# Eight weight-transfer buffers beside the experts in place of six

## The chip, the cores and the metric

The kernel runs on one core of one Trainium2 chip. The time is device microseconds (us) for one execution. Engines are named as in the profile: PE (TensorE matmul), PEld (its weight loads), DVE (VectorE), ACT (ScalarE), POOL (GpSimd) and SP (SyncE, which here issues almost every transfer from device memory).

## What is computed

The reference runs two models one behind the other on a sequence of 256 tokens of width 1024, all in float32. The first block has two layers of attention and a mixture of experts with 32 experts, two of them per token:

```python
def step(acc, ew):
    w1e, w3e, w2e, ge = ew
    h = jax.nn.silu(xt @ w1e) * (xt @ w3e)
    return acc + ge[:, None] * (h @ w2e).astype(f32), None
y, _ = lax.scan(step, jnp.zeros((t, d), f32), (w1, w3, w2, gates.T))
```

Its result feeds the second block: two layers of a hybrid mixer (attention beside a state-space scan) and a gated feed-forward part, on the latent tokens and on 256 context tokens ("ctx"). The context part of layer 0, and the context states of layer 1, do not depend on the first block:

```python
out_l, out_c = hybrid_mixer(h_l, h_c, ..., update_ctx)   # mixer: projections, attention, two scans
x_ctx = x_ctx + g1_c * rmsnorm(m_c, norm_mix_post[l])    # only for l = 0
f_c = rmsnorm(x_ctx, norm_ffn_pre[l]) * (1.0 + sc2_c) + sh2_c
x_ctx = x_ctx + g2_c * rmsnorm(swiglu(f_c, w_gate[l], w_up[l], w_down[l]), norm_ffn_post[l])
```

## The kernel before

**Stages.** The program computes attention of the first block's layer 0 (to about 195 us of the profile), that layer's experts (about 205 to 795), attention of layer 1 (to about 985), its experts (about 990 to 1700), and then the second block on the latent tokens ("the tail", to 2475). A routing step ahead of each expert stage sorts the experts by their number of tokens. A flag chooses at run time between two versions of the stage. The profiled execution takes the one called with `fast` true; only that one is spoken of here.

**An expert stage.** It runs over ten units. A unit is a tile of 128 token slots with one to four experts. For each, `gather` builds a selection matrix `P` on DVE (out of `eq`) and multiplies the tokens `xh`, `xl` by it on PE in two halves of 16 products (`xgp`), each copied by ACT into one half of `xg`. Then `up` runs `h<-wch,xg` for `w1` and again for `w3`, `act` makes `g`, `down` turns `g` on PE (`gtp`), copies it on DVE to `gT`, runs `o<-wch,gT` with `w2`, and adds the result to the tokens by a matrix `St` (`yp`, then `y`). The tiles `gT` and `St` have two buffers each, `eq` has one of its own, and `tmp` (also `tj`) has one.

**Beside the experts.** The ctx pass of the second block runs in pieces between the expert products: `step` is called behind each group of expert products and advances the generator `ctx_pass`. In layer 0 that is the mixer of ctx, in layer 1 its feed-forward part and the states of the next mixer. Its weights (`w_in`, `w_out`, `w_gate`, `w_up`, `w_down`) come through the same buffers as the experts' weights; ACT and DVE split each into two parts (`whi`, `wlo`, lines 152 and 154), and then its buffer is free.

**Transfer buffers.** All large weights come through buffers of [128, 2048] float32, 8 KB in each of 128 partitions or 1.05 MB. `chunk()` hands them out in turn: four of pool `wch`, two of pool `wchm`, which exists up to the end of the second expert stage. A buffer of expert weights is filled by two transfers of 512 KB, a buffer of the ctx pass by one of 1024 KB. SP issues them in program order, and each waits there until the products that read the buffer's former contents are done. So does whatever stands behind it on SP. The built program also names eight completion semaphores (DMAHW0 to DMAHW7), which the transfers use in turn: a transfer waits until the former one on its semaphore has landed. Between the transfers SP also loads the experts' ranks into registers (`value_load`, `TENSOR_LOAD order` in the program), each once a layer.

**Order.** The source gives the order of work and the dependences; a scheduler then sets the order of instructions on each engine, so buffers that are handed out otherwise can change that order.

**Tiles around it.** `res` holds two tiles of 8 KB, `xa` and `xb`. `xb` first holds the ctx input, in attention the sum `pre` (line 299; `x1` in `build`), and beside the experts `m`, the ctx pass's results. `X[0]` is the latent residual of the second block, written first behind the last expert stage; the scan of ctx uses half of it for `y`. `kept[l]` holds the keys, values and two scan states of ctx in layer l, four tiles. `xs` and `Bt` are the scan's inputs.

Of the kernel before, what the change touches and what calls it, by code (L numbers as in the profile page):

```python
# [6 lines left out]
F32 = mybir.dt.float32  # L7
F32R = mybir.dt.float32r
# [55 lines left out]
class Net:  # L64
    def __init__(self, tc, ins, out):
        self.tc, self.nc, self.I, self.out = tc, tc.nc, ins, out
        self.stack = ExitStack()
        self.consts = self.pool("consts")
        self.wch = self.pool("wch", 4)
        self.more = None  # L70
        self.turn = 0
        self.behind = []

# [28 lines left out]


    def chunk(self):
        self.turn = (self.turn + 1) % 3
        p = self.more if self.more is not None and self.turn == 0 else self.wch
        return p.tile([128, 2048], F32, name="wch", tag="wch")

    def row(self, pool, src, name):
        n = src.shape[-1]  # L110
# [470 lines left out]
    def setup2(self):  # L581
        nc, cp, I = self.nc, self.consts, self.I
        V = nc.vector

        self.tri = cp.tile([128, 2, 128], F32, name="tri")
        V.tensor_scalar(self.tri[:, 0], self.iota_f, self.iota_p, None, op0=OP.is_ge)
        V.tensor_scalar(self.tri[:, 1], self.iota_f, self.iota_p, None, op0=OP.is_le)
        self.mask = cp.tile([128, 2, 128], BF, name="mask")
        V.tensor_scalar(self.mask, self.tri, 1.0, -NEG, op0=OP.subtract, op1=OP.mult)
        self.identb = cp.tile([128, 128], BF, name="identb")  # L590
        V.tensor_copy(self.identb, self.ident)
        self.bo = cp.tile([128, 2], F32, name="bo")
        V.tensor_scalar(self.bo[:, 1:2], self.iota_p, 63.5, None, op0=OP.is_gt)
        V.tensor_scalar(self.bo[:, 0:1], self.iota_p, 63.5, None, op0=OP.is_lt)
        self.cols = cp.tile([128, 2, 180], F32, name="cols2")
        nc.gpsimd.dma_start(self.cols, I["c_cols"].rearrange("l p c -> p l c"))
        self.rc = cp.tile([128, 2], F32, name="rcx")
        self.mods = [cp.tile([128, 48, 2], F32, name=f"mod{l}") for l in range(2)]
        self.X = [cp.tile([128, 8, 256], F32, name=f"X{s}") for s in range(2)]
        self.kept = [{"kn": cp.tile([128, 256], F32, name=f"kn{l}"), "v": cp.tile([128, 2, 128], F32, name=f"v{l}"),  # L600
                      "st": [cp.tile([128, 512], F32, name=f"st{l}{d}") for d in range(2)]} for l in range(2)]

    def transpose_in(self, ps, src, s):
        nc = self.nc
# [318 lines left out]
    def mixer(self, l, s, e, m, states_only=False):  # L923
# [24 lines left out]
        mp = self.pool(e.name + f"m{l}", stack=ms)  # L948
# [67 lines left out]
            exps.append(A.activation(dte, dte, AF.Exp).ins)  # L1016


        bc = mp.tile([128, 2, 2, 256], F32, name="bc", tag="bc")
        BT, CT = bc[:, 0], bc[:, 1]  # L1020
        Bt = mp.tile([128, 2, 2, 128], F32, name="Bt")
        xs = mp.tile([128, 2, 512], F32, name="xs")

        def conv(c0, p, out, dst):

# [60 lines left out]
        p = self.gemm2(e, w_in(1280 + 512), h, second=e.second, late=lag)  # L1086
# [3 lines left out]
        for c in range(2):  # L1090
            xc = e.tmp().rearrange("p (k t) -> p k t", k=2)
            p = self.gemm2(e, w_in(1280 + 256 * c), h, second=e.second)
# [3 lines left out]
        if not states_only:  # L1096
            p = self.gemm2(e, w_in(1280 + 768), h, second=e.second)
# [135 lines left out]
        if not states_only:  # L1233

            zs = self.X[0][:, 4:8].rearrange("p (t k) c -> p t (k c)", t=2) if s else mp.tile([128, 2, 512], F32, name="zs")
            for c in range(2):
                ws = self.block(e, w_in(768 + 256 * c))
                p = e.bank("acc", [128, 2, 256])
# [10 lines left out]
        if s:  # L1249
            kn, v = kept["kn"], kept["v"]  # L1250
        else:
            kn = mp.tile([128, 256], F32, name="kn")
            v = mp.tile([128, 2, 128], F32, name="v")
        kvw = self.block(e, w_in(512))
        p = e.bank("acc", [128, 512])
# [13 lines left out]
        if not states_only:  # L1269
# [4 lines left out]
            for c in range(2):  # L1274
                p = self.gemm2(e, w_in(c * 256), h)
# [91 lines left out]
        if m is None:  # L1367
            m = mp.tile([128, 8, 256], F32, name="m1")
        ss = None
        for c in range(4):  # L1370
            p = self.gemm2(e, ("w_out_2", l, 0, 8, c * 256), (ch, cl), order=(4, 5, 6, 7, 0, 1, 2, 3))
# [149 lines left out]
    def experts(self, l, r, xh, xl, y, norm, fast, bg):  # L1521
# [3 lines left out]
        nm = f"moe{l}{'f' if fast else 'g'}"  # L1525
        with ExitStack() as es:
            rp = self.pool(nm + "r", stack=es)
            wk = self.pool(nm + "w", 2, stack=es)
            ps = self.pool(nm + "p", 1, PSUM, stack=es)
            step = bg(es)  # L1530

            sc = r.sc if fast else self.slots(r, rp, False)
            cols = r.cols
# [58 lines left out]

            def gather(t):
                P = wk.tile([128, 2, 128], F32R, name="P", tag="P", bufs=1)
                eq = wk.tile([128, 2, 128], F32, name="eq", tag="eq", bufs=1)
                for tt in range(2):
                    V.tensor_scalar(eq[:, tt], self.iota_f, sc[:, 0, tt, t:t + 1], None, op0=OP.is_equal)
                    V.scalar_tensor_tensor(P[:, tt], self.iota_f, sc[:, 1, tt, t:t + 1], eq[:, tt], op0=OP.is_equal, op1=OP.add)
                xg = wk.tile([128, 8, 128], F32, name="xg", tag="xg", bufs=2 if fast else 3)
                for k0 in range(0, 8, 4):  # L1600
                    p = ps.tile([128, 512], F32, name="xgp", tag="o", bufs=no)
                    for k in range(4):
                        o = p[:, k * 128:(k + 1) * 128]
                        for i, (tt, part) in enumerate(((0, xh), (0, xl), (1, xh), (1, xl))):
                            PE.matmul(o, part[:, tt, k0 + k, :], P[:, tt], start=i == 0, stop=i == 3, skip_group_check=True)  # L1605
                    A.copy(xg[:, k0:k0 + 4, :], p.rearrange("p (k t) -> p k t", k=4))  # L1606
                return xg
# [31 lines left out]
            def down(u, gs_, final):  # L1639
                ts, parts = u  # L1640
                gTs, Ss, gates = [], [], []
                for t, g in zip(ts, gs_):
                    p = ps.tile([128, 512], F32, name="gtp", tag="t", bufs=1)
                    for j in range(4):
                        PE.transpose(p[:, j * 128:(j + 1) * 128], g.rearrange("s (p j) -> s j p", j=4)[:, j], self.ident)
                    gT = wk.tile([128, 4, 128], F32, name="gT", tag="gT")
                    V.tensor_copy(gT, p.rearrange("p (j s) -> p j s", j=4))
                    gTs.append(gT)
                    St = wk.tile([128, 256], F32R, name="St", tag="St")
                    tmp = wk.tile([128, 256], F32, name="tmp", tag="tmp", bufs=1)  # L1650
                    b = 128.0 * t
                    V.tensor_scalar(tmp, rows[:, 0], b, None, op0=OP.is_equal)
                    V.scalar_tensor_tensor(St, rows[:, 1], b, tmp, op0=OP.is_equal, op1=OP.add)
                    gc = wk.tile([128, 3], F32, name="gc", tag="gc")
                    for j in range(2):
                        tj = wk.tile([128, 256], F32, name="tj", tag="tmp", bufs=1)
                        V.scalar_tensor_tensor(tj, rows[:, j], b, rows[:, 2 + j], op0=OP.is_equal, op1=OP.mult,
                                               accum_out=gc[:, j:j + 1])
                    V.tensor_tensor(out=gc[:, 2:3], in0=gc[:, 0:1], in1=gc[:, 1:2], op=OP.add)
                    Ss.append(St)  # L1660
                    gates.append(gc[:, 2:3])
# [3 lines left out]
                for j0 in range(0, 4, nr):  # L1665
                    cs = load(w2v, ranks, slice(j0, j0 + nr), D)
                    first = together([lambda i=i, j=j, dh=dh, k=k, o=o, n=n: PE.matmul(  # L1667
                        os2[dh][i][o:o + n], gTs[i][:, j0 + j, o:o + n], cs[k][:, j, dh * 512:(dh + 1) * 512],
                        start=j0 + j == 0, stop=j0 + j == 3, skip_group_check=True)
                        for i in range(len(ts)) for j in range(nr) for dh in range(2) for k, o, n in reversed(parts)])  # L1670
# [18 lines left out]
            for i, u in enumerate(units):  # L1689
# [6 lines left out]
                    xgs = [gather(t) for t in units[i + 1][0]]  # L1696
                down(u, gs_, i == len(units) - 1)
            step(None)


M_BANKS = {"acc": ("acc", 2), "tr": ("acc", 2), "tp": ("acc", 2), "s": ("acc", 2), "ar": ("acc", 2), "y": ("acc", 2), "yi": ("acc", 2),
# [5 lines left out]
def build(tc, ins, out):  # L1707
    net = Net(tc, ins, out)
    nc = tc.nc
    V, A, PE = nc.vector, nc.scalar, nc.tensor  # L1710
    with net.stack:
        tail = ExitStack()
        with ExitStack() as first:
            res = net.pool("res", stack=first, side="right")
            x = res.tile([128, 2, 1024], F32, name="x", tag="xa")
            for tt in range(2):
                nc.sync.dma_start(x[:, tt], ins["x"][0, tt * 128:(tt + 1) * 128, :])
            cx = res.tile([128, 2, 1024], F32, name="cx", tag="xb")
            net.more = net.pool("wchm", 2, stack=first, side="right")
            net.setup()  # L1720
            net.setup2()
            fnorm = None
            for l in range(2):
                with ExitStack() as es:
                    with ExitStack() as right:
# [6 lines left out]
                        mp = net.pool(f"moe{l}", stack=es)  # L1732
# [23 lines left out]
                        (nc.gpsimd if tt else V).tensor_tensor(out=xl[:, tt], in0=src, in1=f(xh[:, tt]), op=OP.subtract)  # L1756
                    y = res.tile([128, 2, 1024], F32, name="y", tag="xa")
                    A.activation(y, x1, AF.Copy, scale=ALPHA)
                    m = res.tile([128, 8, 256], F32, name="m", tag="xb")

                    def ctx_pass(e):

# [36 lines left out]
                    with cmp.Else():  # L1799
                        net.experts(l, r, xh, xl, y, fnorm, False, lambda es: lambda first, n=0: None)  # L1800
                        with ExitStack() as es2:
                            e = net.env(f"d{l}", es2, T_BANKS, 6, 2)
# [2 lines left out]
                                pass  # L1805
                net.ln_finish(fnorm)
                x = y
            net.more = None

            e = net.env("t", tail, T_BANKS, 12, 4, {"raw": 3, "xdt": 2})  # L1810
            e.other = net.mod_units(1, 8, 24, e.tmp, lambda n: e.bank(n, [128, 512]), True)
            g, b = (net.cols[:, 1, 164 + 8 * i:172 + 8 * i] for i in range(2))
# [21 lines left out]
        with tc.tile_pool(name="ops", bufs=4, space=PSUM) as ps:  # L1834
            for tt in range(2):
                for k0 in range(0, 8, 4):
                    p = ps.tile([128, 512], F32, name="otp", tag="tp")
# [81 lines left out]
```

## Time and profile before

| | before |
|---|---|
| runs | 2459.08, 2465.37, 2470.23 us (median 2465.37) |
| profiled execution, its own time | 2476.79 us |
| its span | 2475.0 us |
| PE busy | 2167.9 us (88%) |
| PEld busy | 1633.0 us (66%) |
| DVE busy | 1097.7 us (44%) |
| ACT busy | 788.5 us (32%) |
| moved from and to device memory | 648.32 MB, mean 262 GB/s |

The span is the time from the first to the last record of the profiled execution; its own time is 1.8 us longer. Busy shares are means over stages that are unlike each other: attention and tail are mostly products, the expert stages are where most of the bytes come in. 744 transfers of 512 KB are expert weights.

### The profile page before, as it was taken

How to read it: one execution, taken by the hardware profiler on the slowest of the kernel's cores; microseconds unless marked ns; L12 is line 12 of the kernel's file. 1: busy time of each engine (PE TensorE's matmuls, PEld its weight loads, DVE VectorE, ACT ScalarE, POOL GpSimd, SP SyncE). 2: the span in 40 equal slices, each digit the busy share in tenths (PEclk: the TensorE clock that was granted, in tenths of full speed). 3: DMA queues.
4: the chain of work that ended last, by engine and by line, in shares of the span. 5: the costliest groups of instructions: out<-in, count | busy, mean ns of one | idle time of the engine just before them, and what ended most of it. 6: DMA issues, size and time to landing. Idle time of an engine off the chain costs nothing.

```text
span 2475.0 us, 40772 instructions
## 1 busy us (share of the span) xinstructions
PE 2167.9 (88%) x16468; PEld 1633.0 (66%) x16468; DVE 1097.7 (44%) x2031; ACT 788.5 (32%) x1309; POOL 143.8 (6%) x133
## 2 busy tenths in 40 slices
PE   7998888788875898798988878787999999999998
PEld 7885444334342887565554545456988998988998
DVE  4456332234322535432323223437755554765553
ACT  4344211122210454312221112214444443634442
POOL 2111000000001121000000000002000001100000
PEclk9998889999998899899999899998999998999999
DMA  9758999999999550999999989895326656405652
GB/s 296 241 170 275 396 345 353 397 409 385 366 356 352 165 170 23 328 365 337 383 377 383 360 320 372 320 361 180 109 68 188 188 175 194 150 5 170 188 179 77
DMA packets 353823, 648.32 MB, mean 262 GB/s; under 512 B 20637, under 2 KB 254181, under 8 KB 352080
## 3 DMA queue, kind: packets, MB, share of 16 engines
q1 hardware_dynamic: 347168, 638.65, 72.2%
q0 software_dynamic: 2288, 6.76, 1.0%
q8 instruction: 133, 2.18, 0.4%
q10 hardware_dynamic: 4160, 0.13, 0.1%
q14 instruction: 74, 0.61, 0.1%
HBM read 644.41 MB, written 1.06 MB: 261 GB/s over the span
## 4 chain that ended last, share of the span: by engine, by line
PE 60%; DMA 17%; issue 14%; DVE 5%; ACT 2%; SPq 1%; POOL 1%; ACTq 0%; DVEq 0%; POOLq 0%
DMA wch<-in_moe_w_dram 16%; PE acc_ps L166 9%; PE acc_ps L167 8%; PE acc_ps L168 8%; PE h L1627 6%; PE o L1667 3%; PE xgp L1605 3%; PE pj L166 3%; PE pj L168 3%; PE pj L167 3%; PE s_ps L1304 1%; PE o_ps L1332 1%; SPq L1565 1%; PE acc_ps L724 1%; PE modmo L643 1%
## 5 line engine op out<-in xcount | busy, mean ns | idle before, releaser
L154 DVE TENSOR_TENSOR wlo<-wch,whi 128x1024 fp32r<-128x1024 f32 (+1 forms) x333 | 403.3, 1213 | 602.1 <-ACT whi L152 579.4
L152 ACT CAST whi<-wch 128x1024 fp32r<-128x1024 f32 x342 | 351.8, 1033 | 720.5 <-PE acc_ps L167 497.2
L1627 PE MATMUL h<-wch,xg 128*32 128x512 f32 (+1 forms) x2368 | 347.6, 668 | 117.2 <-DMA wch<-in_moe_w_dram 117.0
L166 PE MATMUL acc_ps<-hh,whi 128*128 128x256 f32 x1360 | 391.0, 287 | 0.0
L167 PE MATMUL acc_ps<-hl,whi 128*128 128x256 f32 x1360 | 385.7, 284 | 0.0
L168 PE MATMUL acc_ps<-hh,wlo 128*128 128x256 f32 x1360 | 383.9, 282 | 0.0
L166 PEld LDWEIGHTS acc_ps<-hh,whi 128*128 128x128 f32 x1360 | 260.3, 191 | 29.1 <-issue 25.7
L1627 PEld LDWEIGHTS h<-wch,xg 128*32 128x32 f32 (+1 forms) x2368 | 78.7, 118 | 297.7 <-issue 146.0
L167 PEld LDWEIGHTS acc_ps<-hl,whi 128*128 128x128 f32 x1360 | 260.1, 191 | 4.5 <-issue 4.1
L168 PEld LDWEIGHTS acc_ps<-hh,wlo 128*128 128x128 f32 x1360 | 259.4, 191 | 0.8 <-issue 0.4
L1667 PE MATMUL o<-wch,gT 128*32 128x512 f32 (+1 forms) x1184 | 164.0, 635 | 40.7 <-DMA wch<-in_moe_w_dram 39.4
L166 PE MATMUL acc_ps<-ah,whi 128*128 128x256 f32 x528 | 150.7, 285 | 0.0
L167 PE MATMUL acc_ps<-al,whi 128*128 128x256 f32 x528 | 149.5, 283 | 0.0
L168 PE MATMUL acc_ps<-ah,wlo 128*128 128x256 f32 x528 | 148.5, 281 | 0.0
L1667 PEld LDWEIGHTS o<-wch,gT 128*32 128x32 f32 (+1 forms) x1184 | 38.7, 115 | 117.4 <-issue 66.2
L166 PEld LDWEIGHTS acc_ps<-ah,whi 128*128 128x128 f32 x528 | 101.1, 191 | 14.2 <-issue 14.1
L167 PEld LDWEIGHTS acc_ps<-al,whi 128*128 128x128 f32 x528 | 101.3, 192 | 0.0
L168 PEld LDWEIGHTS acc_ps<-ah,wlo 128*128 128x128 f32 x528 | 101.0, 191 | 0.1
L1684 DVE TENSOR_TENSOR y<-y,yp 128x512 f32<-128x512 f32 x80 | 54.6, 686 | 98.9 <-PE yp L1682 98.7
L1605 PE MATMUL xgp<-P,xh 128*128 128x128 f32 x320 | 81.8, 295 | 12.4 <-ACT xg L1606 9.1
L1605 PEld LDWEIGHTS xgp<-P,xh 128*128 128x128 f32 x320 | 65.6, 205 | 30.3 <-ACT xg L1606 23.1
L166 PE MATMUL pj<-xh,whi 128*128 128x256 f32 x256 | 75.6, 296 | 6.0 <-DVE xl L235 4.4
(728 smaller groups left out, 3801.2 us busy)
## 6 DMA issues: line engine op xcount, KB each, us to landing
wch<-in_moe_w_dram SPq DMA_DIRECT2D x744, 512.0 KB, 8.5
wch<-in_w_mod_dram SPq DMA_DIRECT2D x48, 1024.0 KB, 5.3
wch<-in_w_gate_dram SPq DMA_DIRECT2D x33, 1024.0 KB, 6.5
wch<-in_w_up_dram SPq DMA_DIRECT2D x33, 1024.0 KB, 5.6
wch<-in_w_in_dram SPq DMA_DIRECT2D x25, 1024.0 KB, 7.7
wch<-in_w_down_dram SPq DMA_DIRECT2D x24, 1024.0 KB, 5.2
wch<-in_moe_w_dram SPq DMA_DIRECT2D x12, 1024.0 KB, 10.0
wch<-in_w_out_dram SPq DMA_DIRECT2D x12, 1024.0 KB, 5.3
```

Source lines behind the costliest of these rows:

```text
L152: self.copied = nc.scalar.copy(hi, wk).ins
L154: self.halved = E.tensor_tensor(out=lo, in0=wk, in1=f(hi), op=OP.subtract).ins
L166: PE.matmul(out, ah, bh, start=first, stop=False, skip_group_check=True)
L167: PE.matmul(out, ah, bl, start=False, stop=False, skip_group_check=True)
L168: return PE.matmul(out, al, bh, start=False, stop=last, skip_group_check=True).ins
L643: PE.matmul(p[32 * g:32 * g + 32, (c % 2) * 256:(c % 2) * 256 + 256], self.sc[:, 4 * i + g, :], w[:, 4 * i + g, :], start=i == 0, stop=i = ...
L724: self.nc.tensor.matmul(p[:, j], ws[k][a][:, j * 128:(j + 1) * 128], act[b][:, k], start=n + k + j == 0, stop=n == 2 and k == 7, skip_grou ...
L1304: PE.matmul(ss_[c][:, i * 256:(i + 1) * 256], qn[r, j, qt * 128:(qt + 1) * 128], kk[r, :], start=True, stop=True, skip_group_check=True)
L1605: PE.matmul(o, part[:, tt, k0 + k, :], P[:, tt], start=i == 0, stop=i == 3, skip_group_check=True)
L1627: first = together([lambda i=i, q=q, k=k, o=o, n=n: PE.matmul(hs[i][o:o + n], xgs[i][:, k0 + q, o:o + n], cs[k][:, q, :], start=k0 + q == ...
L1667: first = together([lambda i=i, j=j, dh=dh, k=k, o=o, n=n: PE.matmul(os2[dh][i][o:o + n], gTs[i][:, j0 + j, o:o + n], cs[k][:, j, dh * 512 ...
L1684: V.tensor_tensor(out=ys, in0=ys, in1=yp, op=OP.add)
```

## The change

`chunk()` now goes through a list `ring` of places. Up to the end of the second expert stage it has six entries, as before: four times pool `wch`, and `m0` and `m1`. Within the fast version of an expert stage two more are appended, a tile of a new pool and the tile `xb` of `res`, and the turn starts over at the first entry; behind the stage the list has six entries again. In the tail it holds `wch` alone, as before.

To make room, `m` lies in `X[0]`; in layer 0 of the ctx pass `xs` and `Bt` lie in the tiles that will keep layer 1's scan states, keys and values, which become one tile each; in the fast version `gT` and `St` have one buffer each, and `eq` shares the buffer of `tmp`.

```diff
-        self.more = None
+        self.ring = [(self.wch, "wch")]
...
     def chunk(self):
-        self.turn = (self.turn + 1) % 3
-        p = self.more if self.more is not None and self.turn == 0 else self.wch
-        return p.tile([128, 2048], F32, name="wch", tag="wch")
+        self.turn += 1
+        pool, tag = self.ring[self.turn % len(self.ring)]
+        return pool.tile([128, 2048], F32, name="wch", tag=tag)
...
-        self.kept = [{"kn": cp.tile([128, 256], F32, name=f"kn{l}"), "v": cp.tile([128, 2, 128], F32, name=f"v{l}"),
-                      "st": [cp.tile([128, 512], F32, name=f"st{l}{d}") for d in range(2)]} for l in range(2)]
+        self.kept = []
+        for l in range(2):
+            kv = cp.tile([128, 2, 256], F32, name=f"kv{l}")
+            st = cp.tile([128, 2, 512], F32, name=f"states{l}")
+            self.kept.append({"kv": kv, "kn": kv[:, 0], "v": kv[:, 1].rearrange("p (t e) -> p t e", t=2), "both": st,
+                              "st": [st[:, d] for d in range(2)]})
...
+        xs = self.kept[1]["both"] if s and not states_only else mp.tile([128, 2, 512], F32, name="xs")
         BT, CT = bc[:, 0], bc[:, 1]
-        Bt = mp.tile([128, 2, 2, 128], F32, name="Bt")
-        xs = mp.tile([128, 2, 512], F32, name="xs")
+        if s and not states_only:
+            Bt = self.kept[1]["kv"].rearrange("p t (g n) -> p t g n", g=2)
+        else:
+            Bt = mp.tile([128, 2, 2, 128], F32, name="Bt")
...
             step = bg(es)
+            usual = self.ring
+            if fast:
+
+                deep = self.pool(nm + "d", 1, stack=es)
+                self.ring = usual + [(deep, "d"), (self.res, "xb")]
+                self.turn = -1
...
-                eq = wk.tile([128, 2, 128], F32, name="eq", tag="eq", bufs=1)
+                eq = wk.tile([128, 2, 128], F32, name="eq", tag="tmp", bufs=1)
...
-                    gT = wk.tile([128, 4, 128], F32, name="gT", tag="gT")
+                    gT = wk.tile([128, 4, 128], F32, name="gT", tag="gT", bufs=1 if fast else 2)
...
-                    St = wk.tile([128, 256], F32R, name="St", tag="St")
+                    St = wk.tile([128, 256], F32R, name="St", tag="St", bufs=1 if fast else 2)
...
             step(None)
+            self.ring = usual
...
-            net.more = net.pool("wchm", 2, stack=first, side="right")
+            more = net.pool("wchm", 1, stack=first, side="right")
+            net.ring = [(net.wch, "wch")] * 4 + [(more, "m0"), (more, "m1")]
...
-                    m = res.tile([128, 8, 256], F32, name="m", tag="xb")
+                    m = net.X[0]
...
-            net.more = None
+            net.ring = [(net.wch, "wch")]
```

What the change does to the order of instructions is seen at two places. The first is SP's queue at the start of layer 0's experts. Before, six buffers are asked for (two of the first experts, one of `w_in`, three more), and the rank loads follow:

```order
L1565 DMA wch_2505<-in_moe_w1_dram 128x1024
L1565 ISA
L1565 DMA wch_2516<-in_moe_w1_dram 128x1024
L1565 ISA
L1565 DMA wch_2516<-in_moe_w1_dram 128x1024
L1555 TENSOR_LOAD order_2013
L1555 ISA x2
L1555 TENSOR_LOAD order_2013
L1555 ISA x2
```

Of the changed kernel, the same place, with the buffers at its end:

```order
L1579 DMA wch_2512<-in_moe_w1_dram 128x1024
L1579 ISA
L1579 DMA wch_2515<-in_moe_w1_dram 128x1024
L1579 ISA
L1579 DMA wch_2515<-in_moe_w1_dram 128x1024
L125 DMA wch_2584<-in_w_in_2_dram 128x8x256
L1569 TENSOR_LOAD order_2009
L1569 ISA x2
L1569 TENSOR_LOAD order_2009
L1569 ISA x2
```

One more buffer of experts (`wch_2515`) and the second one of `w_in` (`wch_2584`) now stand ahead of the rank loads; before, eight rank loads stood ahead of that `w_in` buffer. Farther on in the stage SP's order is the same but for moves by one or two buffers.

The second place is PE's queue at the end of a unit of layer 0, around `gtp`. Before, 16 products of a gather (the first half for a later unit) stand between `gtp` and the first `o`; here are the last rows ahead of `gtp` and the first of those 16:

```order
L1605 MATMUL xgp<-P,xh 128x128
L1605 MATMUL xgp<-P,xl 128x128
L1645 MATMUL gtp<-ident,g 128x128 x4
L1605 MATMUL xgp<-P,xh 128x128
L1605 MATMUL xgp<-P,xl 128x128
L1605 MATMUL xgp<-P,xh 128x128
```

Of the changed kernel, the same place:

```order
L1619 MATMUL xgp<-P,xh 128x128
L1619 MATMUL xgp<-P,xl 128x128
L1659 MATMUL gtp<-ident,g 128x128 x4
L1681 MATMUL o<-wch,gT 32x512 x8
L166 MATMUL acc_ps<-hh,whi 128x256
L167 MATMUL acc_ps<-hl,whi 128x256
```

The `o` products now stand right behind `gtp`. The 16 products that stood between are a half earlier: one half of a gather stands between `h` products of the unit, the other ahead of `gtp`. Before, 15 of the 20 units have those 16 products (in one case three of them) between `gtp` and `o`; in 11 of them the change takes them out of that place.

## Rows read from the trace of the kernel before

**Rows 1.** The page's 40 equal slices of the span: PE's busy tenths, and GB/s.

```profile
PE   7998888788875898798988878787999999999998
GB/s 296 241 170 275 396 345 353 397 409 385 366 356 352 165 170 23 328 365 337 383 377 383 360 320 372 320 361 180 109 68 188 188 175 194 150 5 170 188 179 77
```

**Rows 2.** Stretches: each engine's busy us, then PE clock, DMA share, GB/s.

```profile
205.00:795.00 590.00, 482.04 (x3342) 255.13 (x3342) 191.27 (x412) 116.09 (x218) 8.64 (x9) 0.92 0.97 368
990.00:1700.00 710.00, 588.32 (x4251) 368.18 (x4252) 250.73 (x446) 159.06 (x220) 10.61 (x13) 0.92 0.94 349
495.00:595.00 100.00, 88.70 (x683) 44.83 (x684) 37.14 (x72) 20.55 (x47) 1.64 (x1) 1.00 1.03 409
```

**Rows 3.** Waits of PE, 205 to 795 us: us in total, times, longest.

```profile
PE h L1627 <- DMA wch<-in_moe_w_dram: 53.9, 35, 4.0
PE o L1667 <- DMA wch<-in_moe_w_dram: 25.8, 11, 4.7
```

**Rows 4.** Waits of PE, 990 to 1700 us.

```profile
PE h L1627 <- DMA wch<-in_moe_w_dram: 63.2, 26, 6.9
PE o L1667 <- DMA wch<-in_moe_w_dram: 13.7, 8, 3.5
```

**Rows 5.** Waits of SP's transfers, whole span.

```profile
SPq L1565 <- PE h L1627: 189.7, 72, 8.9
SPq L1565 <- PE o L1667: 127.4, 49, 14.4
SPq L1565 <- DMA wch<-in_moe_w_dram: 107.8, 142, 3.1
SPq L1565 <- DVE wlo L154: 97.2, 18, 7.3
```

**Rows 6.** Stretches of layer 0's experts below full rate, columns as in rows 2.

```profile
315.00:325.00 10.00, 9.72 (x37) 4.29 (x40) 1.44 (x2) 0.69 (x1) 0.00 (x0) 1.00 0.46 139
380.00:390.00 10.00, 9.69 (x80) 5.62 (x83) 3.89 (x4) 4.33 (x5) 0.00 (x0) 1.00 0.91 307
425.00:430.00 5.00, 5.00 (x47) 2.29 (x50) 1.72 (x3) 1.73 (x4) 0.00 (x0) 1.00 0.35 109
610.00:630.00 20.00, 17.60 (x103) 7.15 (x104) 2.91 (x10) 3.15 (x11) 0.00 (x0) 0.74 0.79 270
675.00:690.00 15.00, 14.21 (x110) 9.99 (x102) 4.62 (x6) 3.55 (x5) 0.00 (x0) 0.89 0.61 224
```

**Rows 7.** Waits of SP's transfers, 675 to 692 us and 425 to 432 us.

```profile
SPq L1565 <- PE h L1627: 16.2, 2, 8.9
...
SPq L1565 <- DVE wlo L147: 8.1, 1, 8.1
```

**Rows 8.** Waits of PE, 675 to 780 us, and 610 to 675 us (last row).

```profile
PE o L1667 <- DMA wch<-in_moe_w_dram: 13.5, 6, 4.7
PE h L1627 <- DMA wch<-in_moe_w_dram: 11.9, 5, 4.0
...
PE h L1627 <- DMA wch<-in_moe_w_dram: 3.1, 1, 3.1
```

**Rows 9.** Stretches of layer 1's experts below full rate, columns as in rows 2.

```profile
1060.00:1070.00 10.00, 9.18 (x78) 7.14 (x80) 5.98 (x10) 3.37 (x5) 0.00 (x0) 1.00 0.87 309
...
1110.00:1125.00 15.00, 14.58 (x73) 8.23 (x73) 3.21 (x8) 1.64 (x3) 0.00 (x0) 1.00 0.69 236
...
1590.00:1605.00 15.00, 14.23 (x94) 7.43 (x93) 7.00 (x16) 7.86 (x13) 0.00 (x0) 1.00 0.34 119
1630.00:1640.00 10.00, 6.90 (x58) 3.87 (x57) 6.01 (x10) 3.34 (x5) 0.00 (x0) 1.00 0.79 289
```

**Rows 10.** SP's issues in order of time: start us, us.

```profile
216.14 0.86 SPq L1565 DMA_DIRECT2D wch<-in_moe_w_dram  x2
...
222.90 0.39 SPq L125 DMA_DIRECT2D wch<-in_w_in_dram  x1
```

**Rows 11.** Waits on tile gT, both expert stages, by releaser.

```profile
  DVE gT L1647: 4.4, 6
```

**Rows 12.** Waits of DVE, whole span.

```profile
DVE y L1684 <- PE yp L1682: 98.7, 61, 6.6
```

## What bounds it, and what the change should do

> **What bounds the kernel now.** I read the slices first. PE is busy for most of the span, but the rate of transfers has two plateaus of 320 to 409 GB/s, one for each expert stage, and there PE's tenths drop to 7 and 8 [rows 1]. In attention and the tail the rate is far lower and PE does not wait for it, and the change leaves the number of buffers there as it was. So I looked only at the two expert stages.
>
> By stretches, layer 0's experts take 590 us at 368 GB/s with PE busy 482.0 us, layer 1's 710 us at 349 GB/s with PE busy 588.3 us. Between 495 and 595 us the rate was 409 GB/s for 100 us on end, so that is what the transfers can do here [rows 2]. At 409 the stages' bytes (590 us at 368 GB/s are 217 MB, 710 at 349 are 248 MB) would take 531 and 606 us: the transfers lose 59 us in one stage and 104 us in the other against their own full rate. PE for its part waits for expert weights: 53.9 + 25.8 = 79.7 us in layer 0 and 63.2 + 13.7 = 76.9 us in layer 1 [rows 3, 4]. Neither engine is the bound all the time. They take turns: PE is busy with ctx pieces while the transfers stand still, and later PE drains what is there and waits.
>
> Why the transfers stand still is in SP's waits. Its expert transfers wait for the `h` and `o` products that still read a buffer, 189.7 and 127.4 us, and 97.2 us for DVE's split of a ctx weight; another 107.8 us, 142 waits of at most 3.1 us, is for the landing of the transfer eight before [rows 5]. The last is what a full queue looks like. The first three cost nothing while transfers are still under way, and everything when none are. So I cut both stages into steps of 5 us and looked for those below full rate. In layer 0 there are, behind the start, six such stretches, five of them in the rows [rows 6]: at 315 to 325 us the rate is 139 GB/s while PE is 97% busy. What SP waits for in them is a buffer: 16.2 us for `h` products around 680, 8.1 us for DVE's `wlo` around 425 [rows 7].
>
> **What two more buffers are worth.** A buffer holds 1.05 MB, which takes 2.56 us at 409 GB/s, two take 5.1 us. A stretch in which SP waits for a buffer and no transfer is under way gets shorter by at most 5.1 us, by no more than the time that is lost in it, and it pays only as far as PE later waits for expert weights before the buffers are full again. So for each stretch I take the smallest of three numbers: time lost in it (its length times 1 - rate/409), 5.1 us, and PE's wait for expert weights up to the next stretch.
>
> Layer 0: 315 to 325 loses 10 x (1 - 139/409) = 6.6, so 5.1. 380 to 390 loses 2.5. 425 to 430 loses 3.7. 610 to 630 loses 6.8, but PE waits only 3.1 us up to 675, so 3.1. 675 to 690 loses 6.8, and PE waits 25.4 us behind it, so 5.1 [rows 6, 8]. The sixth, 455 to 460, gives 1.2. Sum 20.7 us.
>
> Layer 1: sixteen stretches from 1060 to 1640, the first and the last in the rows; the two largest lose 6.3 us (1110 to 1125) and 10.6 us (1590 to 1605) [rows 9]. Neighbours between which PE does not wait count as one, with 5.1 us for both. The same minimum gives 36.0 us, against 76.9 us of waits there. Together 56.7 us.
>
> **The start of each stage.** Here SP waits for no buffer but loads ranks: eight loads lie between 217.0 and 222.9 us, 0.74 us each [rows 10], and nothing new is asked for meanwhile. In the changed order one buffer of experts and one of `w_in` stand ahead of these loads, so up to 5.1 us of transfers run beneath them. Whether PE gains from it is bounded by 0 and 5.1 us a layer. PE is at work in the first products there, and waits later; I take the middle, 5 us for both layers.
>
> **What is given up for room.** With one buffer, `gT` and `St` of a unit must wait for the former unit's `o` and `yp` products. In program order on PE those stand ahead of the unit's last `h` products, so both are free by then, and DVE writes `St` behind the `y` additions as now: I cost this at nothing; it is covered by the 16 and more `h` products between, and without them it would be one `y` step of DVE a unit. `eq` in the buffer of `tmp` binds a gather to the former unit's `tmp` and `tj`, which are on DVE too, in order: no wait across engines, but it moves gathers, and that shows in the order. In 11 units nothing stands between `gtp` and `o` any more, so PE waits for DVE's copy of `gT`. Where that is so today, PE waits 4.4 us in 6 units, 0.73 us each [rows 11]; 11 x 0.73 = 8 us. From below it costs nothing (where PE would have waited for weights anyway), from above it is DVE's longest queue, 6.6 us a unit (rival 3). I take the 8 us in full.
>
> `xb` as a place in the ring waits, at its first use in a stage, until `xh`, `xl` and `y` have been made of `pre`. All three are done ahead of the first `h` products, which need `xh`; `xb` is the eighth buffer asked for. Nothing, covered by seven buffers ahead of it; with that cover gone it would be one buffer's transfer, 2.56 us a layer. The new pool's tile waits in the same way for attention's tiles. `m` in `X[0]`, `xs` and `Bt` in the kept tiles and the joined `kn`/`v` and state tiles change addresses, not work; their former contents are read out before (`y` of the scan by the halves that `w_out` multiplies) or don't exist yet. SP's queue is otherwise the same but for moves by a buffer or two, and each extra buffer adds no transfer.
>
> **Sum.** 56.7 + 5 - 8 = 54 us: some 20 in layer 0 (590 to 570 us), 34 in layer 1 (710 to 676 us). The profiled execution's own time is 2476.8 us, of that 1.8 outside its span, and would be 2423. It lies 11.4 us above the median of the runs, 2465.4; against that I predict **2411 us**. Behind it layer 0 is nearly bound by its transfers (531 us of 570), layer 1 by PE with its other waits (710 - 77 = 633 of 676).
>
> **A rule that speaks against it.** The row is 409 GB/s over 100 us, and 368 and 349 over the stages [rows 2]. The Trainium skill, "DMA: Bandwidth & Descriptors", section "Where 436 GB/s comes from", says that for transfers from device memory the memory side binds, at about 358 GB/s for a core. By that rule 217 MB need 606 us, more than layer 0 takes now, and two more buffers would give nothing. The trace disagrees with it, by 51 GB/s for 100 us. The same page has 425 GB/s for one core alone.
>
> **Rivals.**
>
> 1. *Only one of the two buffers is won.* The other holds a ctx weight that SP now asks for earlier in terms of buffers, and that waits for its split (the 97.2 us of [rows 5] are such). Then the cap is 2.56 us in place of 5.1: 13.9 + 24.9 = 39 us, less 8: 31 us, 2434 us. For it: the order shows `w_in` moved up. Against: it was asked for at the end of the same stretch before.
> 2. *No change.* The transfers' mean cannot rise: what is not lost in standing still is lost in slower transfers, since 409 GB/s was seen only in one stretch without large ctx transfers. Then the time is that of now, 2465 us; the 8 us of `gT` lie in waits that stay. For it: most slices of the stages read 320 to 397 GB/s [rows 1]. Against: the stretches of [rows 6] lie far below even that, and SP's waits name buffers. The rule above of the Trainium skill would make this the outcome.
> 3. *Slower.* A half gather now stands in the middle of `h`. PE works in order, so if DVE has not made `P` (behind `tmp`, `tj` and whatever ctx work it has), the expert products behind it wait with their weights in place. DVE's own waits for `yp` are 98.7 us in 61, the longest 6.6 [rows 12]. In 11 units 6.6 us each is 73 us, and 54 - 73 is a loss of 19: 2484 us. It decides from 4.9 us a unit on; a mean of all those waits is 1.6.
> 4. *More.* `gT`'s waits are all hidden and both starts give their 5.1 us: 56.7 + 10 = 67 us, 2398; with waits in between that the steps of 5 us don't resolve, down to 2385.
>
> **How the numbers follow.** Chances: the forecast (2395 to 2430) 0.50, rival 1 (to 2450) 0.22, no change 0.13, slower 0.07, more 0.08. The predicted time is that of the forecast. Leaving out slower and most of no change gives 2385 to 2460 for 8 in 10. About 0.5%, 12 us, is what a measurement of this kernel can tell from no change; below 2453 lie the forecast, rival 4 and nearly all of rival 1: faster 0.79, same 0.14, slower 0.07.
>
> **What would show it.** Right: the mean rate in the expert stages rises to about 380 and 366 GB/s; PE's waits for expert weights fall from 157 to about 100 us; SP's waits for `h` and `o` fall; the stretches below full rate become fewer, not only later. PE's waits for `gT` rise to about 12 us in 17. Attention and tail keep their length within a few us. Wrong: PE waits for `xgp` behind DVE's `P` in the middle of `h` (rival 3), SP's waits for `wlo` grow (rival 1), or stages as long as now with transfers that take longer at a full queue (rival 2).

## The result

The changed kernel takes 2395.65 us (median of 4 runs, 2391.69 to 2399.19) against 2467.25 us of the kernel before on the same chip (4 runs, 2459.08 to 2470.23): ratio 0.971, 95% interval 0.969 to 0.974, 71.6 us less. The profiled execution took 2391.69 us with a span of 2389.9 us, 85.1 us less than the one before; 13 of these 85 are scatter between executions (that of before lies above its median, this one below).

The 40 slices of the changed kernel, PE's busy tenths and GB/s:

```profile
PE   7998889788876997989988888869999999999998
GB/s 300 240 193 291 389 393 401 397 408 407 394 385 335 159 153 45 367 399 362 399 395 394 394 400 393 367 258 159 72 101 176 183 176 188 141 1 194 186 182 74
```

Against [rows 1] the plateaus are higher and flatter: where 345 and 353 stood in layer 0, and 337, 320 and 320 in layer 1, most slices now read 385 to 408. Attention and the tail read as before. By the profiles, the flag of layer 1 is read 38.8 us earlier (986.3 and 947.5 us), and the last `o` product then follows after 633 us in place of 685. The tail from there is 5 us longer.

The transfers, by stretches (the last column is GB/s): first the kernel before, start and body of each expert stage, then the changed kernel, the same.

```profile
196.00:245.00 49.00, 45.02 (x354) 31.92 (x346) 29.62 (x85) 18.65 (x32) 4.47 (x3) 0.82 0.82 266
245.00:780.00 535.00, 435.48 (x3040) 224.14 (x3040) 161.64 (x328) 101.15 (x189) 8.64 (x9) 0.93 0.99 377
986.00:1025.00 39.00, 32.62 (x200) 25.42 (x204) 25.84 (x77) 15.63 (x21) 0.00 (x0) 0.74 0.76 255
1025.00:1665.00 640.00, 537.76 (x3938) 332.06 (x3930) 204.51 (x336) 135.99 (x185) 3.28 (x5) 0.94 0.96 360
```

```profile
194.00:245.00 51.00, 46.79 (x374) 32.81 (x370) 29.59 (x79) 20.57 (x33) 4.48 (x3) 0.83 0.92 323
245.00:750.00 505.00, 423.94 (x3037) 223.50 (x3028) 165.13 (x337) 99.68 (x188) 8.64 (x9) 0.95 1.02 397
947.00:986.00 39.00, 32.45 (x200) 25.27 (x204) 24.14 (x68) 15.69 (x21) 0.00 (x0) 0.75 0.87 303
986.00:1575.00 589.00, 523.34 (x3946) 329.23 (x3938) 207.60 (x346) 137.91 (x187) 3.29 (x5) 0.96 1.02 389
```

What the transfers lose in a stretch is its length times (1 - rate/409). Before, that is 17.1 + 41.9 + 14.7 + 76.7 = 150.4 us; now 10.7 + 14.8 + 10.1 + 28.8 = 64.4. The 86.0 us between them lie near the 85.1 of the spans. That is arithmetic, not proof: as long as a stage moves the same bytes (455 MB in the four stretches before, 458 now), its length is these bytes at 409 GB/s plus the loss. The loss says where the time lies; what took it away is for the experiments.

Waits in the changed kernel, whole span (us in total, times, longest), first PE's with its busy time, then those of SP's transfers:

```profile
PE o L1681 <- DMA wch<-in_moe_w_dram: 40.4, 16, 5.3
PE h L1641 <- DMA wch<-in_moe_w_dram: 31.8, 18, 5.0
PE xgp L1619 <- DVE P L1612: 13.7, 10, 2.9
PE yp L1695 <- DVE y L1698: 11.4, 15, 1.0
PE o L1681 <- DVE gT L1661: 9.2, 13, 0.8
PE 2142.5 (90%) x16468; PEld 1631.6 (68%) x16468; DVE 1098.5 (46%) x2031; ACT 789.8 (33%) x1311; POOL 144.0 (6%) x133
```

```profile
SPq L1579 <- DMA wch<-in_moe_w_dram: 245.4, 325, 2.4
SPq L1579 <- PE h L1641: 76.5, 44, 7.4
SPq L1579 <- DVE wlo L154: 59.4, 15, 7.5
SPq L1579 <- PE o L1681: 33.8, 20, 5.4
```

PE waits for expert weights 72.2 us in place of 156.6 [rows 3, 4]. SP waits for products 110 us in place of 317, and more than twice as long for the landing of the transfer eight before [rows 5]: the queue is full more often, and a free buffer is far less often what is missing. PE's waits for `P`, `y` and `gT` have grown; before, they were these:

```profile
PE xgp L1605 <- DVE P L1598: 1.9, 2, 1.0
PE yp L1681 <- DVE y L1684: 6.7, 10, 0.8
PE o L1667 <- DVE gT L1647: 1.1, 2, 0.8
```

PE's own account of the 85.1 us closes as well, but only with all of its terms: 84.4 us less waiting for weights and 25.4 us less busy time (2167.9 us before, for as many products), against 24.6 us more waiting for `P`, `y` and `gT`. The products took less time in total while the mean granted clock of the span was 0.946, against 0.938 before.

### The profile page after: what moved, and what is told of

Its sections match the earlier page's. It is cut to its first block, busy times and chain, and to the rows that moved or that the text cites. A ratio compares the mean times of both kernels' runs of the same rounds, so it can differ in the third digit from the quotient of the medians.

```text
span 2389.9 us, 40785 instructions
## 1 busy us (share of the span) xinstructions
PE 2142.5 (90%) x16468; PEld 1631.6 (68%) x16468; DVE 1098.5 (46%) x2031; ACT 789.8 (33%) x1311; POOL 144.0 (6%) x133
## 4 chain that ended last, share of the span: by engine, by line
PE 61%; DMA 14%; issue 14%; DVE 6%; ACT 2%; SPq 1%; POOL 1%; ACTq 0%; DVEq 0%; POOLq 0%
DMA wch<-in_moe_w_dram 13%; PE acc_ps L166 9%; PE acc_ps L167 9%; PE acc_ps L168 9%; PE h L1641 7%; PE pj L166 3%; PE pj L168 3%; PE pj L167 3%; PE o L1681 2%; PE xgp L1619 2%; PE s_ps L1312 1%; PE o_ps L1340 1%; SPq L1579 1%; DVE wlo L154 1%; PE ss_ps L759 1%
## 5 line engine op out<-in xcount | busy, mean ns | idle before, releaser
L1641 PE MATMUL h<-wch,xg 128*32 128x512 f32 (+1 forms) x2368 | 325.2, 635 | 32.2 <-DMA wch<-in_moe_w_dram 31.8
L1619 PE MATMUL xgp<-P,xh 128*128 128x128 f32 x320 | 83.1, 298 | 21.0 <-DVE P L1612 13.7
L1619 PEld LDWEIGHTS xgp<-P,xh 128*128 128x128 f32 x320 | 65.7, 205 | 46.7 <-ACT xg L1620 16.8
L1619 PE MATMUL xgp<-P,xl 128*128 128x128 f32 x320 | 80.3, 289 | 0.0
## 6 DMA issues: line engine op xcount, KB each, us to landing
wch<-in_moe_w_dram SPq DMA_DIRECT2D x744, 512.0 KB, 10.1
```

The source lines that it names most:

```text
L1641: first = together([lambda i=i, q=q, k=k, o=o, n=n: PE.matmul(hs[i][o:o + n], xgs[i][:, k0 + q, o:o + n], cs[k][:, q, :], start=k0 + q == ...
```

## The experiments

Two theories at first. D: the depth of the ring is the whole gain; the tiles that were made smaller cost a little. G: a part comes from the half gathers, which the smaller tiles moved in between `h` products, where PE would have waited for weights. Medians of the kernel before were 2467.4 and 2467.0 us in the two rounds of runs that follow.

**Six places, with the room kept (e1_six_room).**

```diff
-                self.ring = usual + [(deep, "d"), (self.res, "xb")]
+                self.ring = usual
```

> The changed kernel with six places in the ring beside the experts, as before; all that made room stays (one buffer of gT and of St, eq in the buffer of tmp, m in X[0], xs and Bt in the kept tiles), and with it the changed order of the gathers. Theory D (the two buffers are all of the gain, the room costs the 8 us of waits for gT): 2467 to 2476 us, ratio 1.000 to 1.004. Theory G (a part of the gain comes from the half gathers that now stand within the h products, where PE would have waited): 2440 to 2455 us, ratio 0.990 to 0.995. Theory N (the room edits cost nothing): 2465 to 2469.

Measured: 2472.53 us, ratio 1.002 (0.999 to 1.004). D's range, though the interval takes in N's too; G falls. The gathers stand in this program as in the changed one. Its waits of PE, whole span, and PE's busy time:

```profile
PE h L1640 <- DMA wch<-in_moe_w_dram: 76.1, 36, 5.2
PE o L1680 <- DMA wch<-in_moe_w_dram: 39.7, 20, 4.6
PE xgp L1618 <- DVE P L1611: 16.9, 11, 2.9
PE yp L1694 <- DVE y L1697: 12.0, 15, 1.4
PE o L1680 <- DVE gT L1660: 9.2, 13, 0.8
PE 2184.7 (88%) x16468; PEld 1642.5 (66%) x16468; DVE 1098.9 (44%) x2031; ACT 787.5 (32%) x1309; POOL 146.1 (6%) x133
```

Here is a trap in reading waits: PE waits 41 us less for weights than in the kernel before (115.8 against 156.6), and not one microsecond is gained. The half gathers do fill waits, as G has it; but PE waits 28 us more for `P`, `gT` and `y`, and it is busy 16.8 us longer, with a mean granted clock of 0.928 in this execution against 0.938. Together that is 45 us against 41, and this span is 5.0 us longer. The transfers lose at least what they lost: by the two rows below, 40.6 and 86.1 us in the bodies of the stages, 41.9 and 76.7 before.

```profile
245.00:780.00 535.00, 446.65 (x3048) 230.25 (x3040) 165.95 (x340) 100.63 (x189) 5.71 (x5) 0.90 0.98 378
1025.00:1665.00 640.00, 537.23 (x3871) 328.85 (x3870) 202.50 (x335) 135.36 (x185) 2.28 (x4) 0.92 0.95 354
```

**Seven places (e2_seven_room).** The line reads `self.ring = usual + [(self.res, "xb")]`, and the new pool is left out.

> The changed kernel with seven places (xb added, the new pool left out). Theory D by the prediction's minimum with a cap of 2.56 us: 39 us, less 8: 2435 us, ratio 0.987, so half or more of the whole gain of 71.6 us. If buffers count alike (linear): 36 us less, 2431. If the first one does nearly all: below 2412, ratio 0.978. If the second one does: above 2450.

Measured: 2414.45 us, ratio 0.978 (0.974 to 0.982): 53 us less than before, 58 less than with six. Neither the cap of one buffer's transfer (39 us less 8) nor equal worth: the first buffer gives 58 of the 77 us between six places and eight, three quarters. In the bodies of its stages the transfers lose 21.0 and 48.5 us:

```profile
245.00:750.00 505.00, 426.20 (x3013) 224.05 (x3006) 161.32 (x332) 100.77 (x189) 5.71 (x5) 0.94 1.01 392
980.00:1600.00 620.00, 543.86 (x4068) 342.91 (x4060) 217.97 (x372) 146.84 (x201) 3.29 (x5) 0.96 1.00 377
```

These bodies are not cut at the same distance from the flags and the last products as those above. Counted from the flag to the last `o`, both layers together, the transfers lose 160 us with six places, 92 with seven and 68 with eight, and the stages last 1281, 1214 and 1192 us; the medians fall by 58 and 19.

**Seven places, with the tiles as they were (e3_seven_free).**

```diff
-                eq = wk.tile([128, 2, 128], F32, name="eq", tag="tmp", bufs=1)
+                eq = wk.tile([128, 2, 128], F32, name="eq", tag="eq", bufs=1)
...
-                    gT = wk.tile([128, 4, 128], F32, name="gT", tag="gT", bufs=1 if fast else 2)
+                    gT = wk.tile([128, 4, 128], F32, name="gT", tag="gT")
...
-                    St = wk.tile([128, 256], F32R, name="St", tag="St", bufs=1 if fast else 2)
+                    St = wk.tile([128, 256], F32R, name="St", tag="St")
```

> Seven places as in the run before, but gT and St with two buffers and eq with one of its own, as before the change; in the built program the gathers stand as before the change. Against the run before: theory D, 0 to 8 us faster (PE's waits for gT go from about 9 us to 4, those for P from about 13 to 2); theory G, 10 or more us slower, since the half gathers no longer fill waits within h.

Measured: 2416.4 us, ratio 0.980 (0.975 to 0.984), no difference from the run before that these runs can tell. The waits moved back as expected (`gT` 9.8 us to 1.1, `P` 14.1 to 1.8), and those for weights rose from 86.0 to 113.4 us. G falls here too, and so does the price that D had put on the room.

**Eight places, layer 0's tiles partly as they were (e4_eight_l0free).** In layer 0 `eq` has its own buffer and `St` two.

> The changed kernel with eight places, but in layer 0 eq has its own buffer and St two (gT one), which puts layer 0's gathers back to the order of before. Theory D: PE's waits for P (7.4 us) and for gT (5.1 us) in layer 0 fall, but layer 0 is near the rate of its transfers, so 0 to 6 us faster than the changed kernel: 2390 to 2396, ratio 0.969 to 0.971. Theory G: slower than the changed kernel by 5 to 10 us, ratio 0.974 or more.

Measured: 2399.9 us (6 runs), ratio 0.972 (0.969 to 0.975). That is the changed kernel's time within the intervals. The median lies 4 us above D's range and nearer G's number, but after the two runs before it I read it as no difference.

**Five and four places (e5_five_room, e6_four_room).** The ring beside the experts is `usual[:5]`, or `wch` alone. With D left, the question is the law: Q, that time goes with what the transfers lose, or L, a like worth for each buffer. Both runs also leave the ring at `wch` alone behind a stage:

```diff
-            self.ring = usual
+            self.ring = [(self.wch, "wch")]
```

`wch` alone is four buffers. So in layer 1 `usual` is that one entry, and `usual[:5]` too: the run called five has five places in layer 0 and four in layer 1 and in the attention ahead of it. Its expectation takes it for five in both layers.

> The changed kernel with five places in the ring beside the experts (four of wch and m0), all that made room kept. So far, with that room kept: six places 2472.5 us, seven 2414.5, eight 2395.7; the first buffer added gave 58 us, the second 19. Theory Q (time is what the transfers lose by standing still, and each buffer more removes the larger part of what is left): five places 100 to 170 us above six, 2570 to 2640. Theory L (each buffer is worth its own transfer time at each stop, with a like number of stops): some 40 to 60 us above six, 2510 to 2530.

> The same with four places (wch alone). Four buffers are eight transfers of 512 KB, as many as the completion semaphores let be under way, and a group of h products of four experts holds two buffers while it runs. Theory Q: 250 us or more above six, over 2720; PE waits for weights between most groups. Theory L: 80 to 120 us above six, 2550 to 2590.

Measured: 2633.64 us in the run called five (ratio 1.068, 1.064 to 1.071), 2683.43 us with four (1.090, 1.085 to 1.094). The whole series, room kept. By the profiles, "layer 0" is the time from its flag to the flag of layer 1 (its experts and the attention behind them), "layer 1" that from its flag to the start of the last `o`:

| places | us | PE's waits for expert weights, us | layer 0, us | layer 1, us |
|---|---|---|---|---|
| 4 | 2683.4 | 267.8 | 884.5 | 800.6 |
| 5 in layer 0, 4 in layer 1 | 2633.6 | 242.5 | 821.2 | 798.3 |
| 6 | 2472.5 | 115.8 | 786.4 | 694.7 |
| 7 | 2414.5 | 86.0 | 763.3 | 648.1 |
| 8 | 2395.7 | 72.2 | 752.9 | 633.1 |

The flags and the last `o` of the first two (first and last start, us), four places and then the run called five:

```profile
L1811 SPq TENSOR_LOAD <-flag x2: 287/384/480, 196.5 to 1081.0; - x2
L1680 PE MATMUL o<-wch,gT x1184: 589/593/1063, 279.2 to 1881.6; 128*32 128x512 f32 x193, 128*128 128x512 f32 x5
```

```profile
L1811 SPq TENSOR_LOAD <-flag x2: 285/380/476, 194.1 to 1015.3; - x2
L1680 PE MATMUL o<-wch,gT x1184: 589/592/1063, 274.5 to 1813.6; 128*32 128x512 f32 x193, 128*128 128x512 f32 x5
```

The fifth place shortens layer 0 by 63 us, and layer 1, which did not get it, by 2. In layer 0 the fifth to eighth buffers give 63, 35, 23 and 10 us, each less than the one before. In layer 1 the two from four to six give 106 us together, the seventh 47, the eighth 15. (These are single executions; the last steps are within their scatter.) For four places L's 2550 to 2590 is far too low and Q's "over 2720" too high. The run called five tests neither: that 2633.64 lies in Q's range is chance. Five places in both layers were not measured; if layer 1's 106 us divide as layer 0's 98 do, they would take about 2565 us, an estimate that lies between the ranges of L and Q. GB/s of the 40 slices of the run called five:

```profile
GB/s 291 260 167 300 324 344 362 335 400 378 346 357 257 189 102 142 309 291 317 337 307 334 311 313 285 286 278 284 161 82 119 173 185 185 176 45 129 190 173 89
```

Layer 0's plateau reads 300 to 400 here, layer 1's 278 to 337.

PE's busy time falls along the series as well, for the same 16468 products: 2249.3, 2215.5, 2184.7, 2162.5 and 2142.5 us, while the mean granted clock of the span is 0.898, 0.911, 0.928, 0.939 and 0.946. So of the 290 us between the spans with four places and with eight, 107 are products that took less time; no run here holds the clock fixed.

**The ctx pass behind the experts (e7_six_behind, e8_eight_behind).** In both kernels `step` returns at once, and the whole ctx pass runs behind the last expert product.

```diff
                             if first is not None:
+                                return
                                 done[0] += total * share[n] / (12.0 * (2 * share[2] + share[3] + 6 * share[4]))
```

> The kernel before, with the whole ctx pass put behind the expert products in place of between them (nothing is left out). Slower than before in all, by 150 to 350 us, since its products no longer overlap with transfers; that is not the question. Theory T (transfers stand still because ctx pieces keep PE and buffers busy in turn): in the stretch with expert products alone the transfers run at 400 GB/s or more behind the start, with six buffers. Theory B (six buffers are too few for the expert products themselves): below 390 GB/s there too.

> The changed kernel with the ctx pass behind the expert products in the same way. Theory T: against the run before, the stretches with expert products alone get shorter by 15 us at most in both layers together, of it about 10 from the start of the stages, so the whole ratio between the two is 0.990 to 1.000. Theory B: 40 us or more, ratio 0.985 or less.

Measured: 2773.64 us with six (ratio 1.125, 1.121 to 1.129), 2748.04 us with eight (1.113, 1.110 to 1.117); eight against six 0.991. Stretches with expert products alone, six places, then eight:

```profile
245.00:640.00 395.00, 278.50 (x1768) 96.41 (x1764) 63.69 (x147) 25.14 (x40) 0.00 (x0) 0.87 1.00 397
1200.00:1600.00 400.00, 278.16 (x1808) 93.77 (x1800) 64.16 (x147) 25.13 (x40) 0.00 (x0) 0.91 1.01 399
```

```profile
245.00:640.00 395.00, 279.14 (x1800) 96.47 (x1796) 65.02 (x150) 25.13 (x40) 0.00 (x0) 0.89 1.02 407
1200.00:1600.00 400.00, 281.52 (x1830) 98.61 (x1833) 69.17 (x157) 25.92 (x41) 0.00 (x0) 0.90 1.02 408
```

Without ctx pieces PE is busy 70% of the time, and six buffers already hold 397 and 399 GB/s, a little under T's 400; beside the ctx pass they held 377 and 360. So most of what six buffers lose comes from ctx work that takes PE and buffers in turn with the experts; which of the two counts more, these runs do not separate. But not all: in these 795 us six buffers lose 11.6 + 9.8 us, eight 1.9 + 1.0. Two buffers win some 18 us even without any ctx piece, and T as I had put it (15 us at most, most of it at the start) is too strict.

## Why the prediction was right

The mechanism was the one predicted, and rivals 1 and 2 are out: the transfers' mean rate rose (bodies of the stages 377 to 397 and 360 to 389 GB/s), seven places alone gain more than rival 1 gave eight, and SP's expert transfers wait less for `wlo` (59.4 us, 97.2 before), not more. The size is 71.6 us where 54 were forecast. 2395.65 us is less than 1 us inside the forecast's range, beside rival 4, and rival 4's reasons are nearer to what came: the starts gave 11 us, the steps of 5 us had missed some of the loss, and `gT`'s waits cost little. That the time fell on the forecast's side of the line is luck. The terms below are read from the two profiled executions, whose spans differ by 13 us more than the medians. By its steps:

- *What bounds it.* Right, by e7 and e8 for the larger part: turns between ctx pieces and expert weights. Behind the change layer 0 is nearly bound by its transfers, as forecast: 397 GB/s for 505 us.
- *What two more buffers are worth: 56.7 us.* This is the term that was mis-sized. In the bodies of the stages the loss fell by 27.1 and 47.9 us, 75.0 in all, where the minimum gave 20.7 and 36.0. The working counted only stretches that show in steps of 5 us. In steps of 1 us, those under 250 GB/s lost 66.9 us before and 11.5 now, so standing still gave 55 us, about what was forecast; the other 19 us came from steps that ran slower than 409 without standing still (50.8 us before, 31.5 now), and those had no place in the sum. Why those got fewer no run shows. Whether the cap by PE's wait up to the next stretch holds stays open: over the whole span the waits for weights fell by 84.4 us and the time by 85.1, but e1 shows that such waits can also fall by 41 us with nothing gained. The cap of 2.56 us for one buffer gave 39 us; with seven places the steps under 250 GB/s lost 30.7 us, 36 less than before. That does not refute it; another 13 us came again from the slower steps.
- *The start: 5 us, between 0 and 10.* The loss in the starts fell from 31.8 to 20.8 us, 11.0 us. Between 194 and 245 us the transfers lose 15.0 us with six places and the room (289 GB/s, e1), 12.6 with seven (308 GB/s, e2) and 10.7 with eight; the place of the rank loads was not told apart from the depth.
- *The room: 8 us of waits for `gT`.* PE's own waits for `gT` went from 1.1 us in 2 to 9.2 in 13, 8.1 us more in 11 waits. That the size came out is luck: the row of [rows 11], 4.4 us in 6, adds PE's waits (1.1 in 2) and those of its weight loads (3.2 in 4), so it was not 0.73 us a unit of PE. And the waits cost little: six places with the room are 5 us slower in the medians, with an interval from 1 part in a thousand faster to 4 slower, and with seven places there is no difference. They lie in time in which PE would have waited for weights, the case that the prediction priced at nothing.
- *Rival 3.* The wait for `P` in the middle of `h` is there, 13.7 us in 10 with a longest of 2.9, against 1.9 us in 2 before. At 1.4 us each it stays far under the 4.9 us at which it would have decided.
- *The rule of the Trainium skill* ("DMA: Bandwidth & Descriptors", section "Where 436 GB/s comes from", about 358 GB/s from device memory for a core) does not hold here: the rate was 397 GB/s over 505 us, and 408 over 400 us in e8, with the kernel on one core.

The signs named in advance came, and went farther: PE's waits for expert weights fell to 72 us where about 100 were forecast. By the profiles layer 0 up to the flag of layer 1 got 37.3 us shorter and layer 1 51.5, where 20 and 34 were forecast.

Attention and the tail kept their length within 7 us, the tail being 5 us longer. None of these runs beat the changed kernel; giving the smaller tiles back won nothing (e3, e4), and a ninth place was not tried.

What stays open: what five buffers in both layers take, why there are fewer slow steps that do not stand still, and how the 11 us at the starts divide.

## What to carry to other kernels

Where two streams of work share one ring of transfer buffers, measure the full rate of the transfers in a stretch where nothing stops them, and take from each stage's mean how much they lose against it: that loss, here 118 us in the stages' bodies and 32 in their starts, is the most that more depth can win. With the same bytes the time must follow it, so it does not show the cause; a run with the room given up and the depth as before does (e1). The waits of the engine that consumes are a poor measure by themselves, since other waits and a longer busy time can take their place. The worth of one more buffer falls fast (63, 35, 23 and 10 us in layer 0 here), and the tiles given up for two of them cost next to nothing.

## What was not expected

The waits that the smaller tiles bring (8 us for `gT`, 12 for `P`) cost nothing that can be measured in these kernels. With fewer buffers not only the waits grew but also the products' own time, by 107 us between eight places and four, at a lower granted clock. And the series looked uneven, 50 us from four to five places and 161 from five to six, until the stages were read by layer: the run called five had four places in layer 1.
